# Instance norm in tiles: the last tile's statistics in one pass, and the end wait on another engine

## The chip, the cores and the metric

The kernel runs on one core of a Trainium2 chip. The metric is the device time of one execution in microseconds. A profile's "span" is some 1.7 us less than the time of the same execution. In profile lines PE is TensorE, DVE VectorE, ACT ScalarE, POOL GpSimd and SP SyncE; a q behind the name marks the engine's queue, where a transfer is issued. A transfer "lands" when the record of its end arrives. For the comparisons each kernel was run several times in turn with the kernel before, on the same chip.

Executions of the kernel before fall into two groups: of 59, 35 took 1246.70 to 1247.61 us (mean 1247.01) and 24 took 1249.23 to 1252.50, with nothing in between. I call them the **lower** and the **upper** group, and use the same split, at 1248, for the other kernels.

## The reference

```
mean = np.mean(x, axis=(2, 3, 4), keepdims=True)
var = np.var(x, axis=(2, 3, 4), keepdims=True)
return ((x - mean) / np.sqrt(var + eps)).astype(np.float32)
```

x has the shape (8, 64, 32, 64, 64) in fp32: 512 instances of 131072 elements, 268 MB, read once and written once.

## The kernel before

Two small parts come first, then 42 tiles of 128 partitions by 12288 columns, held in four slots of SBUF. A tile is three chunks of 4096 columns, and one instance is spread over 32 chunk rows; so each statistic is summed by partition, masked by chunk, summed over partitions by a matmul, and handed back to the chunks.

SyncE loads. VectorE and ScalarE each take part of the sums, then part of the squares about the mean, and scale. ScalarE issues the stores. Only the last tile's store goes in two pieces:

```python
    def tile_on_vector(eng, t, lane, c1, c3, c4, c16):
        ...
        for j, part in ((0, chunk[0]), (3, t[:, COLS - TURN :])):      # TURN = 1536
            eng.reduce_sum(out=column(a, SUMS, j), in_=part, axis=AXIS)...
        over_instance(eng, a, p[:, 0:12], SUMS, 4, MEANS, True, ...)   # mask, matmul, reduce, mask, reduce
        eng.tensor_scalar(out=chunk[0], in0=chunk[0], scalar1=column(a, MEANS, 0), ...)
        eng.tensor_tensor_reduce(out=unused[2][:], in0=chunk[0], in1=chunk[0], ..., accum_out=...)
        over_instance(eng, a, p[:, 12:21], SQUARES, 3, VARS, False, ...)
        eng.reciprocal(...)
        ... scale chunk[0], scale and shift chunk[1]

    def tile_on_scalar(eng, t, lane, c1, c3, c4, c16, dst, last=False):
        ... Identity with accum_out over chunk 1 and 2560 columns of chunk 2
        ... Square with bias = -mean and accum_out over chunks 1 and 2, then Sqrt
        if last:
            at = CHUNK
            eng.dma_start(out=dst[:, :at], in_=chunk[0])._wait_ge(done[lane], c3 - 2)...
        eng.activation(out=chunk[2], ..., scale=..., bias=...)
        eng.dma_start(out=dst[:, at:], in_=t[:, at:])._wait_ge(done[lane], c3)...

    def load_all(eng):                       # on SyncE
        ... all loads
        for k in range(n_tiles - SLOTS, n_tiles):
            uses = k // SLOTS + 1 + (k == n_tiles - 1)
            eng.wait_ge(stored[k % SLOTS], 16 * uses)
```

## Time and profile before

| | before |
|---|---|
| time | 1246.93 us, median of 3 (1246.81 to 1247.07) |
| span of the profile | 1245.6 us (its own execution took 1247.35) |
| moved | 536.9 MB, mean 431 GB/s |
| last load landed | 1206.11 us |
| first and second store of the last tile issued | 1225.70, 1229.92 us |
| last landing | 1244.34 us |

The last row is from the trace's records of DMA landings; the others are on the page and in the timeline. The prediction shows the lines and reads them.

### The profile page before, as it was taken

Reading aid. Unit: us, or ns where it says so; the run is one execution under the profiler, and the core shown is the slowest. Engines: PE = TensorE matmul, PEld = TensorE weight load, DVE = VectorE, ACT = ScalarE, POOL = GpSimd, SP = SyncE. Lnnn points to the kernel's source line nnn. Section 1 sums busy time; section 2 is a strip of 40 time slices with the busy share of each in tenths; the row PEclk is TensorE's granted clock in tenths of the full one; section 3 lists DMA queues with packets and bytes.
Section 4 is the critical chain, followed back from the end, with each engine's and each line's share of the span. In section 5 each row is a group of like instructions: output and inputs, shape, how many; then the busy total and the mean of one; then the engine's idle time right before and its main releaser. Section 6 shows DMA issues by size and latency. Waiting matters only on the chain.

```text
span 1245.6 us, 1951 instructions
## 1 busy us (share of the span) xinstructions
PE 52.6 (4%) x176; PEld 44.0 (4%) x176; DVE 811.4 (65%) x724; ACT 757.7 (61%) x433; POOL 2.7 (0%) x15
## 2 busy tenths in 40 slices
PE   0000000000000000000000000000000000000000
PEld 0000000000000000000000000000000000000000
DVE  2887666666666666666666666666666666666663
ACT  5776555666566666655556665666566555566653
POOL 0000000000000000000000000000000000000000
DMA  9999999999999999999999999999999999999998
GB/s 394 429 431 433 445 432 429 431 431 437 439 434 429 429 436 440 432 432 431 431 439 437 432 431 429 434 444 432 432 428 432 437 440 432 429 429 436 442 432 363
DMA packets 12818, 536.89 MB, mean 431 GB/s; under 512 B 1424, under 2 KB 1424, under 8 KB 1424
## 3 DMA queue, kind: packets, MB, share of 16 engines
q1 hardware_dynamic: 6336, 268.44, 49.9%
q10 hardware_dynamic: 6480, 268.44, 49.8%
q14 instruction: 2, 0.02, 0.0%
HBM read 268.44 MB, written 268.44 MB: 431 GB/s over the span
## 4 chain that ended last, share of the span: by engine, by line
another core or an unknown queue 82%; DMA 9%; ACT 3%; DVE 2%; SPq 1%; issue 1%; PE 0%; ACTq 0%
DMA slot<-in_x_dram 6%; DMA out_dram<-slot 4%; ACT unused L221 2%; SPq L364 1%; DVE small L157 1%; DVE slot L193 1%; ACT unused L214 0%; DVE slot L200 0%; ACT slot L240 0%; PE psum L257 0%; DVE small L137 0%; DVE small L125 0%; DVE small L131 0%; DVE small L143 0%
## 5 line engine op out<-in xcount | busy, mean ns | idle before, releaser
L214 ACT ACTIVATE unused<-slot 128x4096 uint8<-128x4096 f32 x84 | 249.3, 2968 | 310.8 <-DMA slot<-in_x_dram 308.4
L157 DVE TENSOR_REDUCE small<-slot 128x1 f32<-128x4096 f32 x84 | 255.3, 3081 | 280.0 <-DMA slot<-in_x_dram 280.0
L221 ACT ACTIVATE unused<-slot,small 128x4096 uint8<-128x4096 f32 x84 | 310.8, 3701 | 65.2 <-DVE small L143 65.2
L171 DVE CUSTOM_DVE_ANT_0 unused<-slot 128x4096 uint8<-128x4096 f32 x42 | 185.9, 4425 | 1.4
L240 ACT ACTIVATE slot<-slot,small 128x4096 f32<-128x4096 f32 x42 | 159.7, 3801 | 21.1 <-DVE small L188 18.0
L200 DVE TENSOR_SCALAR slot<-slot,small 128x4096 f32<-128x4096 f32 x42 | 101.1, 2407 | 0.0
L164 DVE TENSOR_SCALAR slot<-slot,small 128x4096 f32<-128x4096 f32 x42 | 98.8, 2353 | 1.5
L257 PE MATMUL psum<-small,avg 128*128 128x12 f32 (+1 forms) x168 | 50.3, 375 | 1144.6 <-DVE small L125 1144.6
L193 DVE TENSOR_SCALAR slot<-slot,small 128x4096 f32<-128x4096 f32 x42 | 98.6, 2347 | 0.0
L257 PEld LDWEIGHTS psum<-small,avg 128*128 128x128 f32 x168 | 42.0, 310 | 1152.8 <-DVE small L125 1152.8
L131 DVE TENSOR_REDUCE small<-psum 128x3 f32<-128x12 f32 x84 | 14.2, 169 | 58.0 <-PE psum L257 58.0
L228 ACT ACTIVATE small<-small,eps_t 128x3 f32<-128x3 f32 x42 | 12.5, 299 | 62.6 <-DVE small L143 62.6
L125 DVE TENSOR_TENSOR small<-small,belongs 128x12 f32<-128x12 f32 x84 | 14.2, 170 | 31.9 <-ACT unused L221 29.6
L185 DVE RECIPROCAL small<-small 128x3 f32<-128x3 f32 x42 | 7.4, 176 | 15.4 <-ACT small L228 15.4
L137 DVE TENSOR_TENSOR small<-small,belongs 128x9 f32<-128x9 f32 x84 | 14.3, 170 | 2.9
L221 ACT ACTIVATION_READ_ACCUMULATOR unused<-slot,small 128x1 f32 x84 | 15.7, 186 | 0.0
L214 ACT ACTIVATION_READ_ACCUMULATOR unused<-slot 128x1 f32 x84 | 15.6, 186 | 0.0
L143 DVE TENSOR_REDUCE small<-small 128x3 f32<-128x9 f32 x84 | 13.6, 162 | 2.9
L270 DVE TENSOR_REDUCE small<-slot 128x1 f32<-128x2048 f32 x2 | 4.6, 2284 | 9.0 <-DMA slot<-in_x_dram 9.0
L296 ACT ACTIVATE unused<-slot,small 128x4096 uint8<-128x4096 f32 x2 | 7.4, 3707 | 2.0 <-DVE small L273 2.0
L293 ACT ACTIVATE unused<-slot 128x2048 uint8<-128x2048 f32 x2 | 3.8, 1910 | 7.2 <-DMA slot<-in_x_dram 6.7
L188 DVE TENSOR_TENSOR small<-small 128x3 f32<-128x3 f32 x42 | 6.8, 162 | 1.4
(26 smaller groups left out, 21.1 us busy)
## 6 DMA issues: line engine op xcount, KB each, us to landing
slot<-in_x_dram SPq DMA_DIRECT2D x42, 6144.0 KB, 39.9
out_dram<-slot ACTq DMA_DIRECT2D x41, 6144.0 KB, 54.2
out_dram<-slot ACTq DMA_DIRECT2D x3, 2048.0 KB, 23.9
slot<-in_x_dram SPq DMA_DIRECT2D x2, 2048.0 KB, 10.2
out_dram<-slot ACTq DMA_DIRECT2D x1, 4096.0 KB, 14.4
```

What stands on the lines that cost most here:

```text
L125: eng.tensor_tensor(out=block(a, by_both, n, m), in0=spread(a, at, m), in1=belongs[:, :, :m], op=Alu.mult,)._wait_ge(*wait).then_inc(steps ...
L131: eng.tensor_reduce(out=a[:, by_instance : by_instance + n], in_=p.rearrange("p (n m) -> p n m", m=m), axis=AXIS, op=Alu.add,)._wait_ge(st ...
L137: eng.tensor_tensor(out=block(a, by_chunk, n, n), in0=spread(a, by_instance, n), in1=belongs[:, :, :n].rearrange("p i c -> p c i"), op=Alu ...
L157: eng.reduce_sum(out=column(a, SUMS, j), in_=part, axis=AXIS)._wait_ge(landed[lane], c16).then_inc(summed[lane], 1)
L164: eng.tensor_scalar(out=chunk[0], in0=chunk[0], scalar1=column(a, MEANS, 0), scalar2=None, op0=Alu.add,)._wait_ge(centred[lane], c1).then_ ...
L171: eng.tensor_tensor_reduce(out=unused[2][:], in0=chunk[0], in1=chunk[0], scale=1.0, scalar=0.0, op0=Alu.mult, op1=Alu.add, accum_out=colum ...
L193: eng.tensor_scalar(out=chunk[0], in0=chunk[0], scalar1=column(a, SCALES, 0), scalar2=None, op0=Alu.mult,)._wait_ge(scaled[lane], c1).then ...
L200: eng.tensor_scalar(out=chunk[1], in0=chunk[1], scalar1=column(a, SCALES, 1), scalar2=column(a, SHIFTS, 1), op0=Alu.mult, op1=Alu.add,)._w ...
L214: eng.activation(out=unused[j - 1][:, : part.shape[1]], in_=part, func=Act.Identity, accum_out=column(a, SUMS, j),)._wait_ge(landed[lane], ...
L221: eng.activation(out=unused[j - 1][:], in_=chunk[j], func=Act.Square, bias=column(a, MEANS, j), accum_out=column(a, SQUARES, j),)._wait_ge ...
L240: eng.activation(out=chunk[2], in_=chunk[2], func=Act.Identity, scale=column(a, SCALES, 2), bias=column(a, SHIFTS, 2),)._wait_ge(shifted[l ...
L257: eng.matmul(out=p[:, col : col + THIRDS * m], lhsT=avg[PART][:], rhs=a[:, at + m : at + m + THIRDS * m], start=True, stop=True,)._wait_ge ...
```

## The change

Its intent: in the last tile no later load hides the compute, so shorten it. VectorE takes means and variances of chunk 0 and 3360 columns of chunk 1 in one pass with bn_stats. ScalarE makes mean and spread of its own columns about its own mean, without waiting for the instance's. Both are combined from four pieces with weights by size. The wait for the last stores moves from SyncE to ScalarE. Cut to its core:

```diff
+    GROUP = 480
+    SHARE = 7 * GROUP
+    sizes = (CHUNK, SHARE, CHUNK, CHUNK - SHARE)
+    def last_on_vector(eng, t, lane, c1, c3, c4, c16):
+        for g, (at, size) in enumerate(groups):          # 8 of 512 columns, 7 of 480
+            i = eng.bn_stats(out=stats[:, g, :], in_=t[:, at : at + size])
+        step(eng.bn_aggr(out=a[:, 0:2], in_=stats[:, :split, :]))
+        step(eng.bn_aggr(out=a[:, 2:4], in_=stats[:, split:, :]))
+        weigh(means, BOTH); hand_out(0, ...)             # weights, matmul, reduce, mask, reduce
+        ... variances + (own mean - instance mean)^2, weigh, hand_out, reciprocal
+        ... scale and shift chunk 0, then chunk 1
+    def last_on_scalar(eng, t, lane, c1, c3, c4, c16, dst):
+        ... Identity with accum_out over 4096 and 736 columns: own means
+        ... Square about the own mean over the same columns, with accum_out
+        ... Sqrt, first store, scale and shift chunk 2, second store
@@ load_all
+    def wait_for_stores(eng):
         for k in range(n_tiles - SLOTS, n_tiles):
@@ set_up
+        ... 6 more small steps on GpSimd: belongs4 and weighs
@@ end
-    over_tiles(nc.vector, part_on_vector, tile_on_vector)
+    over_tiles(nc.vector, part_on_vector, tile_on_vector, last_on_vector)
+    wait_for_stores(nc.scalar)
```

More of the change, by code (lines that the diff above doesn't have):

```diff
@@ L72 @@
     belongs = sbuf("belongs", [P, THIRDS, THIRDS + 1])
+    GROUP = 480
+    SHARE = 7 * GROUP
+    first_of = (0, CHUNK, 2 * CHUNK, CHUNK + SHARE)
+    sizes = (CHUNK, SHARE, CHUNK, CHUNK - SHARE)
+    PIECES = len(sizes)
+    belongs4 = sbuf("belongs4", [P, THIRDS, PIECES])
+    weighs = sbuf("weighs", [P, THIRDS, PIECES])
+    groups = [(i * 512, 512) for i in range(CHUNK // 512)]
+    groups += [(CHUNK + i * GROUP, GROUP) for i in range(SHARE // GROUP)]
+    stats = sbuf("stats", [P, len(groups), 6])
+    late = sbuf("late", [P, 96])
     small = [sbuf(f"small{i}", [P, 72]) for i in range(LANES)]
@@ L97 @@
     moved = semaphores("moved", SLOTS)
+    went, meant, leaned, spread_, multiplied, took_root = semaphores("late", 6)
     sorted2 = semaphores("sorted2", SLOTS)
@@ L207, in tile_on_vector, with tile_on_scalar @@
         )._wait_ge(shifted[lane], c1).then_inc(done[lane], 1)
-    def tile_on_scalar(eng, t, lane, c1, c3, c4, c16, dst, last=False):
+    def tile_on_scalar(eng, t, lane, c1, c3, c4, c16, dst):
         a = small[lane]
@@ L233, in tile_on_scalar @@
         )._wait_ge(gathered[lane], c1).then_inc(rooted[lane], 1)
-        at = 0
-        if last:
-            at = CHUNK
-            eng.dma_start(out=dst[:, :at], in_=chunk[0])._wait_ge(
-                done[lane], c3 - 2
-            ).then_inc(stored[lane], 16)
         eng.activation(
@@ L246, in tile_on_scalar @@
         )._wait_ge(shifted[lane], c1).then_inc(done[lane], 1)
-        eng.dma_start(out=dst[:, at:], in_=t[:, at:])._wait_ge(done[lane], c3).then_inc(
+        eng.dma_start(out=dst, in_=t)._wait_ge(done[lane], c3).then_inc(
             stored[lane], 16
@@ L263, in tile_on_tensor, with step, weigh, hand_out @@
             )._wait_ge(before[lane], c1).then_inc(after[lane], 1)
+    BIAS, BOTH, INST, CHUNKED, NEGATIVE, FAR, FAR2, TOTAL = 8, 10, 22, 25, 37, 41, 45, 49
+    BOTH2, INST2, CHUNKED2, FOUND, ROOTED, SCALED, SHIFTED = 53, 65, 68, 77, 80, 83, 86
+    def last_on_vector(eng, t, lane, c1, c3, c4, c16):
+        a, p = late, psum[lane]
+        n, m = THIRDS, PIECES
+        means, variances = a[:, 0 : 2 * m : 2], a[:, 1 : 2 * m : 2]
+        count = 0
+        def step(i):
+            nonlocal count
+            if count:
+                i._wait_ge(went, count)
+            i.then_inc(went, 1)
+            count += 1
+        def weigh(what, to):
+            step(
+                eng.tensor_tensor(
+                    out=block(a, to, n, m),
+                    in0=what.unsqueeze(1).to_broadcast([P, n, m]),
+                    in1=weighs[:],
+                    op=Alu.mult,
+                )
+            )
+        def hand_out(col, inst, at, to, k, negate):
+            eng.tensor_reduce(
+                out=a[:, inst : inst + n],
+                in_=p[:, col : col + n * m].rearrange("p (n m) -> p n m", m=m),
+                axis=AXIS,
+                op=Alu.add,
+            )._wait_ge(multiplied, 1 if col == 0 else 2).then_inc(went, 1)
+            nonlocal count
+            count += 1
+            step(
+                eng.tensor_tensor(
+                    out=block(a, at, k, n),
+                    in0=a[:, inst : inst + n].unsqueeze(1).to_broadcast([P, k, n]),
+                    in1=belongs4[:, :, :k].rearrange("p i c -> p c i"),
+                    op=Alu.mult,
+                )
+            )
+            step(
+                eng.tensor_reduce(
+                    out=a[:, to : to + k],
+                    in_=block(a, at, k, n),
+                    axis=AXIS,
+                    op=Alu.add,
+                    negate=negate,
+                )
+            )
+        for g, (at, size) in enumerate(groups):
+            i = eng.bn_stats(out=stats[:, g, :], in_=t[:, at : at + size])
+            if g == 0:
+                i._wait_ge(landed[lane], c16)
+        i.then_inc(went, 1)
+        count += 1
+        split = CHUNK // 512
+        step(eng.bn_aggr(out=a[:, 0:2], in_=stats[:, :split, :]))
+        step(eng.bn_aggr(out=a[:, 2:4], in_=stats[:, split:, :]))
+        eng.wait_ge(meant, 2)
+        weigh(means, BOTH)
+        hand_out(0, INST, CHUNKED, NEGATIVE, m, True)
+        step(
+            eng.tensor_add(
+                out=a[:, FAR : FAR + m], in0=means, in1=a[:, NEGATIVE : NEGATIVE + m]
+            )
+        )
+        far = a[:, FAR : FAR + m]
+        step(eng.tensor_mul(out=a[:, FAR2 : FAR2 + m], in0=far, in1=far))
+        eng.wait_ge(spread_, 2)
+        step(
+            eng.tensor_add(
+                out=a[:, TOTAL : TOTAL + m], in0=variances, in1=a[:, FAR2 : FAR2 + m]
+            )
+        )
+        weigh(a[:, TOTAL : TOTAL + m], BOTH2)
+        hand_out(n * m, INST2, CHUNKED2, FOUND, n, False)
+        eng.wait_ge(took_root, 1)
+        step(
+            eng.reciprocal(out=a[:, SCALED : SCALED + n], in_=a[:, ROOTED : ROOTED + n])
+        )
+        step(
+            eng.tensor_mul(
+                out=a[:, SHIFTED : SHIFTED + n],
+                in0=a[:, NEGATIVE : NEGATIVE + n],
+                in1=a[:, SCALED : SCALED + n],
+            )
+        )
+        assert count == STEPS
+        for j in (0, 1):
+            part = t[:, j * CHUNK : (j + 1) * CHUNK]
+            eng.tensor_scalar(
+                out=part,
+                in0=part,
+                scalar1=column(a, SCALED, j),
+                scalar2=column(a, SHIFTED, j),
+                op0=Alu.mult,
+                op1=Alu.add,
+            )._wait_ge(went, STEPS).then_inc(done[lane], 1)
@@ new lines @@
+    WEIGHED, WEIGHED2, VARIED, STEPS = 4, 11, 14, 16
+    def last_on_scalar(eng, t, lane, c1, c3, c4, c16, dst):
+        a = late
+        mine = [(j, t[:, first_of[j] : first_of[j] + sizes[j]]) for j in (2, 3)]
+        for j, part in mine:
+            eng.activation(
+                out=unused[j - 2][:, : sizes[j]],
+                in_=part,
+                func=Act.Identity,
+                scale=1.0 / sizes[j],
+                accum_out=column(a, 0, 2 * j),
+            )._wait_ge(landed[lane], c16).then_inc(meant, 1)
+        for j, _ in mine:
+            eng.activation(
+                out=column(a, BIAS, j - 2),
+                in_=column(a, 0, 2 * j),
+                func=Act.Identity,
+                scale=-(sizes[j] ** -0.5),
+            )._wait_ge(meant, 2).then_inc(leaned, 1)
+        for j, part in mine:
+            eng.activation(
+                out=unused[j - 2][:, : sizes[j]],
+                in_=part,
+                func=Act.Square,
+                scale=sizes[j] ** -0.5,
+                bias=column(a, BIAS, j - 2),
+                accum_out=column(a, 0, 2 * j + 1),
+            )._wait_ge(leaned, 2).then_inc(spread_, 1)
+        eng.activation(
+            out=a[:, ROOTED : ROOTED + THIRDS],
+            in_=a[:, FOUND : FOUND + THIRDS],
+            func=Act.Sqrt,
+            bias=eps_t[:, 0:1],
+        )._wait_ge(went, VARIED).then_inc(took_root, 1)
+        eng.dma_start(out=dst[:, :CHUNK], in_=t[:, :CHUNK])._wait_ge(
+            done[lane], c3 - 2
+        ).then_inc(stored[lane], 16)
+        eng.activation(
+            out=t[:, 2 * CHUNK :],
+            in_=t[:, 2 * CHUNK :],
+            func=Act.Identity,
+            scale=column(a, SCALED, 2),
+            bias=column(a, SHIFTED, 2),
+        )._wait_ge(went, STEPS).then_inc(done[lane], 1)
+        eng.dma_start(out=dst[:, CHUNK:], in_=t[:, CHUNK:])._wait_ge(
+            done[lane], c3
+        ).then_inc(stored[lane], 16)
@@ L268, in part_on_vector, with last_on_tensor @@
+    def last_on_tensor(eng, t, lane, c1, c3, c4, c16):
+        for col, at, ready_at in ((0, BOTH, WEIGHED), (12, BOTH2, WEIGHED2)):
+            eng.matmul(
+                out=psum[lane][:, col : col + THIRDS * PIECES],
+                lhsT=avg[PART][:],
+                rhs=late[:, at : at + THIRDS * PIECES],
+                start=True,
+                stop=True,
+            )._wait_ge(went, ready_at).then_inc(multiplied, 1)
     def part_on_vector(eng, t, lane):
@@ L329, with over_tiles @@
     ]
-    def over_tiles(eng, on_part, on_tile, with_target=False):
+    def over_tiles(eng, on_part, on_tile, on_last, with_target=False):
         for m, (lane, t) in enumerate(parts):
@@ L348, in over_tiles @@
             c = k // SLOTS + 1
-            more = (out_t[k], k == n_tiles - 1) if with_target else ()
-            on_tile(eng, slots[k % SLOTS][:], k % SLOTS, c, 3 * c, 4 * c, 16 * c, *more)
+            more = (out_t[k],) if with_target else ()
+            step = on_last if k == n_tiles - 1 else on_tile
+            step(eng, slots[k % SLOTS][:], k % SLOTS, c, 3 * c, 4 * c, 16 * c, *more)
     def load_all(eng):
@@ L433, in set_up @@
         )
+        for to, c in ((slice(0, THIRDS), slice(0, THIRDS)), (slice(3, 4), slice(1, 2))):
+            step(eng.tensor_copy(out=belongs4[:, :, to], in_=belongs[:, :, c]))
+        for j, size in enumerate(sizes):
+            step(
+                eng.tensor_scalar(
+                    out=weighs[:, :, j : j + 1],
+                    in0=belongs4[:, :, j : j + 1],
+                    scalar1=float(size),
+                    scalar2=None,
+                    op0=Alu.mult,
+                )
+            )
         return count
@@ L438 @@
     nc.vector.wait_ge(ready, set_by)
-    over_tiles(nc.vector, part_on_vector, tile_on_vector)
+    over_tiles(nc.vector, part_on_vector, tile_on_vector, last_on_vector)
     nc.tensor.wait_ge(ready, set_by)
-    over_tiles(nc.tensor, part_on_tensor, tile_on_tensor)
+    over_tiles(nc.tensor, part_on_tensor, tile_on_tensor, last_on_tensor)
     nc.scalar.preload_act_table(Act.Sqrt)
     nc.scalar.wait_ge(ready, set_by)
-    over_tiles(nc.scalar, part_on_scalar, tile_on_scalar, with_target=True)
+    over_tiles(nc.scalar, part_on_scalar, tile_on_scalar, last_on_scalar, with_target=True)
+    wait_for_stores(nc.scalar)
 _INS = ['x', 'eps']
```

## The prediction

> **What bounds the kernel now.** I read first the page's rows of busy tenths, because the change touches one tile of 42 and so only the end of the span.
>
> ```profile
> DVE  2887666666666666666666666666666666666663
> ACT  5776555666566666655556665666566555566653
> DMA  9999999999999999999999999999999999999998
> DMA packets 12818, 536.89 MB, mean 431 GB/s; under 512 B 1424, under 2 KB 1424, under 8 KB 1424
> ```
>
> VectorE and ScalarE are busy six tenths, the DMA engines nine or more in every slice but the last. The kernel moves 536.9 MB and is bound by transfers. So the question is whether the end, where no more loads come, has another limit. The chain that ended last seems to say so: after the last load (landed at 1206.11) it runs through compute only.
>
> ```profile
> 1206.13 6.09 DVE small L157 x2
> ...
> 1213.71 7.50 ACT unused L221 x4
> ...
> 1223.40 2.28 DVE slot L193
> 1225.68 0.02 issue
> 1225.70 0.35 ACTq L237
> 1226.05 0.05 issue
> 1226.09 3.80 ACT slot L240
> ```
>
> The reader sees 19.57 us (1206.13 to 1225.70) from the landing to the first store of the last tile: two passes of sums and squares, 6.09 + 7.50 us, the small steps around them, and the scaling. The change shortens this. But that chain is of instructions, and stops at ScalarE's last one; it doesn't say whether the store, once issued, waits behind older stores. The busy table of the end does:
>
> ```profile
> core 0: us, PE busy (x) PEld busy (x) DVE busy (x) ACT busy (x) POOL busy (x), PEclk, DMA share, GB/s
> 1140.00:1198.96 58.96, 2.40 (x8) 2.00 (x8) 39.07 (x35) 35.31 (x21) 0.00 (x0) 1.00 0.99 430
> 1206.11:1241.20 35.09, 1.20 (x4) 1.00 (x4) 19.13 (x17) 17.62 (x10) 0.00 (x0) 1.00 0.99 427
> 1241.20:1245.60 4.40, 0.00 (x0) 0.00 (x0) 0.00 (x0) 0.00 (x0) 0.00 (x0) 1.00 0.09 37
> ```
>
> From the last landing to 1241.20 the DMA engines are as full (0.99, 427 GB/s) as in the steady part (0.99, 430), though nothing but stores is left. The reason is in the DMA issues:
>
> ```profile
> out_dram<-slot ACTq DMA_DIRECT2D x41, 6144.0 KB, 54.2
> out_dram<-slot ACTq DMA_DIRECT2D x1, 4096.0 KB, 14.4
> ```
>
> A store lands 54.2 us after its issue, while a tile of 6.29 MB needs 14.5 us at 433 GB/s: about two older stores are always queued. Counting the trace's packets from 1206.11 on, 15.14 MB are still to write: 6.29 are the last tile, 8.85 are the backlog of tiles 40 and 41. The backlog takes 8.85 / 0.433 = 20.4 us, to 1226.5. The last tile's first store is issued at 1225.70. Packet by packet, the first DMA engine ends its backlog at 1226.56 and goes on with the new store at once; sorted into 16 chains, no engine has a gap above 0.08 us from 1206 to its end. The compute chain is only just hidden, but it is hidden. The engines end at 1241.2 to 1243.9; the last one, never idle, sets the landing at 1244.34.
>
> **What the Trainium skill says.** "Perfetto Trace Analysis", section "Identifying the Most-Contended Engine", says to find the engine of highest occupancy and optimize that first: here the DMA, 0.99 even in the tail, which the change leaves alone. "DMA: Bandwidth & Descriptors", section "Specifications", gives 435 GB/s as the fabric's ceiling and about 358 as the HBM limit of a core; the trace agrees with the first (430 and 427) and is above the second. Its section "Queues, rings and completion order" says that an engine consumes descriptors in ring order; the trace agrees: packets of the new store start only after an engine's backlog ends. "VectorE: DVE Perf Modes", section "The perf-mode tier table", has tensor_reduce at one element per cycle and fp32 tensor_scalar at two; the trace agrees (4.42 us and 2.35 us for 4096 columns). I found no page with a cost for bn_stats, so I take the rate of tensor_reduce.
>
> **The change part by part** (times of the last tile, from its rows).
>
> VectorE's statistics. Removed: sums of 4096 and 1536 columns (6.09), the centring of chunk 0 (2.35), its squares (4.43) and one scaling of 2.35 that becomes a scale-and-shift (2.41). Added: bn_stats over 4096 + 3360 = 7456 columns in 15 instructions. Reductions of 4096 and 1536 columns take 4.419 and 1.743 us, so 1.045 ns per column and 0.14 us fixed, of which neighbours overlap about 0.08. Estimate: 7456 x 1.045 ns + 15 x 0.06 us = 8.7 us, to 1214.8. Two bn_aggr on small inputs, 0.24 each: 1215.3.
>
> ScalarE's statistics. Identity over 4096 takes 3.62 us and over 2560 takes 2.32, so 736 columns take 0.78; two tiny bias instructions of 0.3; Square over 4096 (3.71) and 736 (about 0.9) with accumulator reads. Sum about 9.8 us: done at 1215.9.
>
> Combining. Mask, matmul, reduce, mask, reduce took 1212.24 to 1213.71, 1.47 us; it is needed twice as before, now with no pass of data between. 1215.3 + 1.47 + two small steps 0.4 = 1217.2; ScalarE is done by then, so no wait. Add 0.2, combine 1.47, square root 0.33, reciprocal and product 0.4: 1219.6. Scaling chunk 0, 2.41: the first store is issued at about 1222.0 in place of 1225.70. ScalarE then scales chunk 2 (0.35 + 3.8), and the second store goes at about 1226.2 in place of 1229.92. So 3.7 us of the compute chain go. **Worth in time: none.** Both stores queue behind a backlog that is untouched, and at 1226.5 the engines go on with the same bytes at the same rate.
>
> Setup. Six GpSimd instructions more. The present ones end at 4.2 us, and take about 0.27 each including the handover; 4.2 + 6 x 0.27 = 5.8, before the first data at 9.02. Hidden.
>
> End wait. SyncE sees the last landing at 1244.36 and leaves 1.3 us of closing work to 1245.65. In the trace the other engines are released by SyncE's signal at 1244.59, and SyncE collects their answers from 1244.755 to 1244.82. With the wait on ScalarE, SyncE should already be in that collection, and only ScalarE's answer is missing. From 1244.39, the answer plus its handover should need about 0.1 where now 0.4 pass. Estimate: 0.3 us less. This is the only part on the path that sets the end.
>
> Sum: 1246.93 - 0 - 0 - 0.3 = **1246.6 us**.
>
> **Rivals.**
> 1. The compute chain sets the end after all; all 3.7 us arrive: 1246.93 - 3.7 - 0.3 = 1242.9. For it speaks the chain of instructions, and that the new store came only just in time. Against it: the share of 0.99 and the chains of packets without gaps. Even with all gaps closed the slowest engine had 37 us of its own packets to move after 1206.9. I give it 3 in 100.
> 2. bn_stats is slower than one column per cycle. At half the rate it takes 16.5 us, the first store goes 7.8 us later than I say, at 1229.8, and the engines stand idle some 4 us: about 1250.5. Nothing in this profile has measured bn_stats; 4 in 100.
> 3. Last DMA engine: one engine ends 1.2 us after the next (landings at 1244.34 and 1243.17). If queueing earlier changes which engine is behind, the end moves by some tenths either way. The same step (1.2 us) is seen at the landing of the store before, so I expect it to stay.
> 4. The end wait saves nothing, as both engines must meet in the closing barrier: 1246.9. Possible, 1 in 4; it lies in the range.
>
> **Range and chances.** The three runs before differ by 0.26 us. With the end wait's 0 to 0.4 and some tenths for rival 3, the range of 8 in 10 is 1245.9 to 1247.2. 2% is 25 us; no rival comes near: within 2% 0.98, the rest split.
>
> **What would show it.** In the changed kernel's timeline the first and second stores of the last tile are issued near 1222.0 and 1226.2, but land where they did, so their times to landing grow from 9.0 and 14.4 us to some 12.7 and 18. The DMA share stays about 0.99 from the last landing to 1241. bn_stats over 512 columns shows about 0.6 us each. The first data are still used at about 9.0 us. The closing work after the last landing shrinks from 1.3 to about 1.0 us. Wrong would make it: a landing of the first store well before 1234, or a gap of the DMA before it.

## The result, and the profile after

In the six first executions each, the changed kernel took 1247.00 us (median; 1246.76 to 1249.58), the kernel before 1246.91 (1246.78 to 1247.13). The ratio is 1.0004, 95% interval 0.9991 to 1.0017: the same. Ratios here are the mean time of one kernel's fast runs over that of the other's of the same rounds, so not quite the ratio of the medians.

The timeline of the changed kernel's last tile (start, duration, engine, line, operation, tiles) shows that the compute did get faster:

```profile
1205.96 8.76 DVE L332 BATCH_NORM_STATS2 stats<-slot 128x6 f32<-128x512 f32 x15 [7.21 <-DMA slot<-in_x_dram]
...
1214.53 0.89 ACT L405 ACTIVATE unused<-slot,late 128x736 uint8<-128x736 f32 x1
1214.75 0.37 DVE L338 BATCH_NORM_AGGREGATE late<-stats 128x2 f32<-128x48 f32 x1
...
1219.90 4.73 DVE L372 TENSOR_SCALAR slot<-slot,late 128x4096 f32<-128x4096 f32 x2
1222.35 0.35 ACTq L419 DMA_DIRECT2D out_dram<-slot  x1
1222.74 3.80 ACT L422 ACTIVATE slot<-slot,late 128x4096 f32<-128x4096 f32 x1 [3.35 <-DVE slot L372]
1226.57 0.34 ACTq L429 DMA_DIRECT2D out_dram<-slot  x1
```

Two passes have become one of 8.76 us on VectorE; ScalarE is through at 1215.5, in time. The stores are issued 3.35 us earlier by the clock of the span. What became of that stands in the landing times. First the changed kernel's issue of the 4 MB store (name, queue, count, size, us to landing), then the first store's line from its source view:

```profile
out_dram<-slot ACTq DMA_DIRECT2D x1, 4096.0 KB, 17.6
```

```profile
DMA to landing us min/median/max: 12.2/12.2/12.2
```

Before, these were 14.4 and 9.0 us. Each store now waits 3.2 us longer for its landing: all that it gained, as the chain from the last load's landing to the first issue is 3.18 us shorter. The busy table of the changed kernel's end, with the last two columns DMA share and GB/s, is the twin of the one before:

```profile
1140.00:1198.78 58.78, 2.40 (x8) 2.00 (x8) 38.89 (x35) 35.24 (x20) 0.00 (x0) 1.00 0.99 430
1205.96:1241.00 35.04, 1.21 (x4) 1.00 (x4) 16.41 (x32) 13.59 (x12) 0.00 (x0) 1.00 0.99 427
1241.00:1245.30 4.30, 0.00 (x0) 0.00 (x0) 0.00 (x0) 0.00 (x0) 0.00 (x0) 1.00 0.07 30
```

VectorE's busy time after the last load fell from 19.13 to 16.41 us and ScalarE's from 17.62 to 13.59, and the DMA share stayed 0.99. The saving was of time that lay beside the transfers.

### The profile page after: what moved, and what is told of

The parts are those of the page before. It is cut to its first block, busy times and chain, and to the rows that moved or that the text cites. A ratio compares the mean times of both kernels' runs of the same rounds, so it can differ in the third digit from the quotient of the medians.

```text
span 1245.3 us, 1977 instructions
## 1 busy us (share of the span) xinstructions
PE 52.7 (4%) x176; PEld 44.1 (4%) x176; DVE 808.7 (65%) x739; ACT 753.7 (61%) x435; POOL 4.0 (0%) x21
## 4 chain that ended last, share of the span: by engine, by line
another core or an unknown queue 82%; DMA 9%; DVE 3%; ACT 2%; SPq 1%; issue 1%; PE 0%; ACTq 0%; DVEq 0%
DMA slot<-in_x_dram 6%; DMA out_dram<-slot 4%; ACT unused L236 1%; SPq L543 1%; DVE stats L332 1%; DVE small L173 0%; ACT unused L229 0%; DVE slot L216 0%; DVE slot L209 0%; ACT slot L422 0%; PE psum L266 0%; DVE slot L372 0%; PE psum L435 0%; SPq L541 0%
## 5 line engine op out<-in xcount | busy, mean ns | idle before, releaser
L229 ACT ACTIVATE unused<-slot 128x4096 uint8<-128x4096 f32 x82 | 243.4, 2968 | 302.9 <-DMA slot<-in_x_dram 300.5
L173 DVE TENSOR_REDUCE small<-slot 128x1 f32<-128x4096 f32 x82 | 249.2, 3081 | 272.8 <-DMA slot<-in_x_dram 272.8
L236 ACT ACTIVATE unused<-slot,small 128x4096 uint8<-128x4096 f32 x82 | 303.4, 3701 | 63.7 <-DVE small L159 63.7
L187 DVE CUSTOM_DVE_ANT_0 unused<-slot 128x4096 uint8<-128x4096 f32 x41 | 181.4, 4426 | 1.4
L249 ACT ACTIVATE slot<-slot,small 128x4096 f32<-128x4096 f32 x41 | 155.9, 3801 | 18.0 <-DVE small L204 18.0
L216 DVE TENSOR_SCALAR slot<-slot,small 128x4096 f32<-128x4096 f32 x41 | 98.7, 2406 | 0.0
L180 DVE TENSOR_SCALAR slot<-slot,small 128x4096 f32<-128x4096 f32 x41 | 96.5, 2353 | 1.5
L266 PE MATMUL psum<-small,avg 128*128 128x9 f32 (+1 forms) x164 | 49.1, 375 | 1116.7 <-DVE small L141 1116.7
L209 DVE TENSOR_SCALAR slot<-slot,small 128x4096 f32<-128x4096 f32 x41 | 96.2, 2346 | 0.0
L332 DVE BATCH_NORM_STATS2 stats<-slot 128x6 f32<-128x512 f32 (+1 forms) x15 | 8.8, 662 | 7.2 <-DMA slot<-in_x_dram 7.2
L390 ACT ACTIVATE unused<-slot 128x4096 uint8<-128x4096 f32 (+1 forms) x2 | 4.4, 2208 | 8.0 <-DMA slot<-in_x_dram 8.0
L474 ACT ACTIVATE unused<-slot,small 128x4096 uint8<-128x4096 f32 x2 | 7.4, 3707 | 2.0 <-DVE small L451 2.0
## 6 DMA issues: line engine op xcount, KB each, us to landing
out_dram<-slot ACTq DMA_DIRECT2D x41, 6144.0 KB, 54.2
```

The source lines that it names most:

```text
L216: eng.tensor_scalar(out=chunk[1], in0=chunk[1], scalar1=column(a, SCALES, 1), scalar2=column(a, SHIFTS, 1), op0=Alu.mult, op1=Alu.add,)._w ...
L229: eng.activation(out=unused[j - 1][:, : part.shape[1]], in_=part, func=Act.Identity, accum_out=column(a, SUMS, j),)._wait_ge(landed[lane], ...
L236: eng.activation(out=unused[j - 1][:], in_=chunk[j], func=Act.Square, bias=column(a, MEANS, j), accum_out=column(a, SQUARES, j),)._wait_ge ...
L249: eng.activation(out=chunk[2], in_=chunk[2], func=Act.Identity, scale=column(a, SCALES, 2), bias=column(a, SHIFTS, 2),)._wait_ge(shifted[l ...
L266: eng.matmul(out=p[:, col : col + THIRDS * m], lhsT=avg[PART][:], rhs=a[:, at + m : at + m + THIRDS * m], start=True, stop=True,)._wait_ge ...
L332: i = eng.bn_stats(out=stats[:, g, :], in_=t[:, at : at + size])
```

## The experiments

My theory: the stores of earlier tiles keep the DMA engines busy until after the last tile's stores are issued, so the last tile's chain has slack, and its length matters only beyond that. Rival A: the chain sets the end. Rival B: the slack is unlimited, as only bytes count. A second question is what the end wait is worth.

The load of the last tile lands at other times in each execution (1205.6 to 1209.1 in the profiles), mostly 2 to 3 us later in the upper group. So profiles of different groups are compared from that landing on. This table gathers them; its columns are worked out from the traces' landing records, the timeline and the span:

| kernel | last load's landing | to the first store's issue | to the end of the span | closing work |
|---|---|---|---|---|
| before | 1206.11 | 19.59 | 39.54 | 1.306 |
| changed | 1205.93 | 16.41 | 39.36 | 1.103 |
| end wait alone | 1208.76 | 19.59 | 39.20 | 1.102 |
| new statistics alone | 1207.85 | 16.41 | 39.56 | 1.306 |
| changed, one extra sum | 1206.81 | 20.22 | 39.40 | 1.103 |
| before, one extra sum | 1209.05 | 23.46 | 40.78 | 1.306 |
| changed, two extra sums | 1205.95 | 24.54 | 41.67 | 1.103 |
| before, store cut | 1205.61 | 19.59 | 36.92 | 1.306 |
| changed, store cut | 1208.24 | 16.41 | 33.54 | 1.102 |

"Closing work" is from the last landing to the end of the span.

The landing records also show what the upper group is. The last load has one landing for each of the 16 DMA engines. In two profiles of the changed kernel, at 1247.00 and 1249.59 us, the mean of these landings is nearly the same, 1203.88 and 1204.09, but the last of them comes at 1205.93 and 1208.65. At the end of the last store it is the same again: means 1241.99 and 1242.20, last 1244.19 and 1246.75. So in the slower execution one engine is further behind, and the others are not. Why it falls behind isn't shown.

### The two halves of the change alone

```diff
# end wait alone: the kernel before, and
+    def wait_for_stores(eng): ...
+    wait_for_stores(nc.scalar)
# new statistics alone: the changed kernel, and
-    wait_for_stores(nc.scalar)
+    wait_for_stores(nc.sync)
```

> The kernel before with the end wait moved from SyncE to ScalarE and nothing else. If the end wait is the only part on the path that sets the end (my theory, as predicted): the closing work after the last landing shrinks from 1.3 us to about 1.1 (1.10 in the profile of the changed kernel), time 0.2 us under the kernel before, 1246.7. Rival: what the closing work gains is inside the noise or is given back outside of the span, time as before within 0.1 us.

> The change with the end wait put back on SyncE: the new statistics alone. Theory (the stores queue behind the backlog): first and second store issued near 1222.3 and 1226.6 as in the changed kernel, landings at about 1234.6 and 1244.3 as before, closing work 1.3 us, time as before within 0.2 us, 1246.9. Rival (the compute chain sets the end): 3.4 us less, 1243.5.

The end wait alone took 1247.29 us (median of 5, 1246.80 to 1249.65), ratio 0.9993 (0.9979 to 1.0007). The new statistics alone took 1248.63 (median of 6, 1247.38 to 1250.01), ratio 1.0004 (0.9991 to 1.0018). Many of these executions were of the upper group, so 0.2 us can't be read from them; but Rival A's 3.4 us can: it is not there. From the landing of the last load to the end the new statistics alone need 39.56 us, the kernel before 39.54, with the first store 3.18 us earlier. The closing work is 1.306 us with the wait on SyncE and 1.102 or 1.103 with it on ScalarE, in all 18 profiles.

The profiles of the upper group sharpen the theory. In the one of the end wait alone, with its old statistics, the last load lands late and so does the first store's issue, at 1228.35 us; most engines have ended their backlog by then and stand idle. In one of the changed kernel (the run at 1249.59 us, reported below) the store is issued at 1225.06, in time. First the end wait alone, then the changed kernel:

```profile
1226.80:1228.20 1.40, 0.00 (x0) 0.00 (x0) 1.40 (x1) 0.00 (x0) 0.00 (x0) 1.00 0.08 35
```

```profile
1226.80:1228.20 1.40, 0.00 (x0) 0.00 (x0) 0.55 (x1) 1.40 (x1) 0.00 (x0) 1.00 0.79 339
```

Both need 39.2 us from the last load's landing to the end, although the share is 0.08 in one and 0.79 in the other. In both the engine that ends last never ran out of packets. So it is this engine that hides the chain, and not that all of them are full.

### Using up the slack

A sum over 4096 columns that nobody reads is put on VectorE ahead of the last tile's scaling:

```diff
# before, one extra sum (last tile only)
+        eng.reduce_sum(out=a[:, 70:71], in_=chunk[0], axis=AXIS)
         eng.reciprocal(out=a[:, SCALES : SCALES + 3], ...)
# changed, one (two) extra sums
+        eng.reduce_sum(out=a[:, 95:96], in_=t[:, :CHUNK], axis=AXIS)
         eng.wait_ge(took_root, 1)
```

> The kernel before with one extra sum over 4096 columns on VectorE ahead of the last tile's scaling, 4.42 us of which some 0.4 hide behind the square root: the first store is issued at about 1229.8 in place of 1225.7. Theory: the engines that end their backlog at 1226.6 stand idle 4 us, but the one that ends last (landing at 1229.8, so its data at 1229.4) idles only from 1229.4 to about 1230.8; the end moves by 1.4 to 2 us, not by 4: about 1248.6. Rival (the compute chain sets the end): plus 4.0 us, 1250.9. A rival of pure backlog, with a lot of slack: no change.

> The changed kernel with the same extra sum of 4.42 us (some 4.0 of it not hidden): first store issued at about 1226.4, so 0.7 us later than in the kernel before. Theory: the 3.4 us that the change saved are slack and are what is used up here; the slowest DMA engine is not reached and the time stays as that of the changed kernel within 0.2 us, 1247.0. Rival (the compute chain sets the end): plus 4.0, 1251.0.

> The changed kernel with two extra sums, 8.84 us of which 8.4 are not hidden: first store at about 1230.8, 5.1 us later than in the kernel before. Theory: the slowest DMA engine, free at about 1229.4, waits until about 1231.8: plus 2.4 us, and the other engines then end at 1246.4 too: 1249.5 to 1250. Rival (the chain sets the end): plus 8.4, 1255.4.

Changed with one extra sum: 1248.16 us (median of 6, 1247.10 to 1249.92), ratio 1.0002 (0.9988 to 1.0016); its two quickest executions, 1247.10 and 1247.18, lie among those of the changed kernel. A chain 3.81 us longer (20.22 against 16.41) moved the end by 0.04 us. Before with one extra sum: 1249.04 (1248.08 to 1251.57), ratio 1.0008 (0.9994 to 1.0022), three of six at 1248.08 to 1248.65. There a chain 3.87 us longer moved the end by 1.24. Changed with two: 1249.32 (1249.27 to 1249.36, all four), ratio 1.0014 (0.9998 to 1.0029): 8.13 us longer, 2.30 us later. So neither rival holds. Not all of the length arrives, against A; and some of it does once the slack is used up, against B.

The busy table of the kernel before with one extra sum shows the slack's end (the last two columns are the DMA share and GB/s):

```profile
1209.00:1226.00 17.00, 1.20 (x4) 1.00 (x4) 14.60 (x14) 13.82 (x9) 0.00 (x0) 1.00 0.98 422
1229.00:1232.00 3.00, 0.00 (x0) 0.00 (x0) 2.97 (x4) 0.00 (x0) 0.00 (x0) 1.00 0.04 16
1233.50:1248.00 14.50, 0.00 (x0) 0.00 (x0) 1.30 (x1) 3.21 (x1) 0.00 (x0) 1.00 0.97 417
```

Now all 16 engines are idle before the first store, which is issued at 1232.51. Sorting the packets into 16 chains, the engines idle between 1.1 and 7.1 us there: most end their backlog at 1226.4 to 1227.3, one only at 1232.28. The 1.1 us of this last one are close to the 1.24 that the end moved, where the others' 4 to 7 us cost nothing more: they would have waited at the end for the last one.

### Taking the backlog away

The store of the last tile but one is cut to 128 of its 12288 columns, in both kernels. Their outputs are wrong, which doesn't matter for the times.

```diff
-        eng.dma_start(out=dst, in_=t)...
+        to = COLS if keep is None else keep          # keep = 128 for tile n_tiles - 2
+        eng.dma_start(out=dst[:, :to], in_=t[:, :to])...
```

> The kernel before, but the store of the last tile but one is cut from 12288 columns to 128 (its output is wrong on purpose), which takes 6.2 MB or 14.4 us of the backlog away. Theory: the queue then runs empty at about 1212 to 1215, long ahead of the first store at 1225.7, so that compute chain sets the end: 6.29 MB from about 1226.7 take 14.5 us to 1241.2, landing near 1241.7, and 1.3 us of closing work: span about 1243.0, time 1244.2 to 1245. It gains only 2 to 3 of the 14.4 us, since the chain was hidden only just. Rival (transfers alone count): 14 us less, 1232.5.

> The changed kernel with the same store cut (output wrong on purpose). Theory: now nothing hides the last tile's chain, so the change is worth what it saves of it: first store at 1222.4 in place of 1225.7, and the time is 3.2 to 3.6 us under that of the kernel before with the same cut: about 1241. Rival (the change is worth nothing even then, for example because the stores themselves are slower): the same time as the kernel before with the cut.

The kernel before with the cut took 1244.24 us (median of 5, 1244.14 to 1244.67), ratio 0.9974 (0.9960 to 0.9988): it lost 14.4 us of transfers and gained under 3. The changed kernel with the cut took 1241.73 in its one execution of the lower kind and 1243.48 to 1244.26 in the other four, median 1243.59, ratio 0.9966 (0.9952 to 0.9979). By the medians the expected 3.2 to 3.6 us are missed: the gain is 0.65. The profile says where the rest is: in it the last load landed at 1208.24, and at 1205.61 in the other kernel's (why, isn't shown). From that landing on, 36.92 us became 33.54: 3.38 less, which are the chain's 3.18 and the closing work's 0.20. First the busy table of the kernel before with the cut, then that of the changed kernel with it:

```profile
1205.60:1212.00 6.40, 0.03 (x1) 0.03 (x1) 6.25 (x3) 6.03 (x4) 0.00 (x0) 1.00 0.91 392
1214.50:1226.00 11.50, 0.60 (x2) 0.50 (x2) 9.61 (x11) 6.91 (x6) 0.00 (x0) 1.00 0.00 0
1226.20:1240.70 14.50, 0.00 (x0) 0.00 (x0) 1.29 (x1) 3.19 (x1) 0.00 (x0) 1.00 0.97 416
```

```profile
1208.20:1212.00 3.80, 0.00 (x0) 0.00 (x0) 3.73 (x7) 3.73 (x3) 0.00 (x0) 1.00 0.99 427
1217.20:1225.00 7.80, 1.21 (x4) 1.00 (x4) 5.57 (x17) 0.93 (x3) 0.00 (x0) 1.00 0.00 0
1225.60:1240.20 14.60, 0.00 (x0) 0.00 (x0) 1.35 (x1) 3.25 (x1) 0.00 (x0) 1.00 0.98 417
```

In both, the engines move nothing for several microseconds (share 0.00) while VectorE and ScalarE work, and then need 14.5 us for the last tile. Here the chain sets the end, and from the last load's landing on the change is worth all that it saves. In the real kernel the same chain lies beside 14.4 us more of stores.

### What became of the end wait's 0.2 us

The closing work is 0.20 us shorter in every profile, yet the changed kernel is not quicker. I ran it and its halves again:

> The changed kernel again, to settle whether the 0.20 us that its closing work is shorter (1.103 us against 1.306 in every profile so far, by where the end wait stands) reach the time. In the undisturbed executions (before: 1246.77 to 1247.14) theory: 0.2 us under before. Rival: no difference, because the time in which the last DMA engine lands scatters by as much.

> The end wait alone, again, for more undisturbed executions. Theory: as the changed kernel, 0.2 us under before. Rival: as before.

> The new statistics alone, again; so far it has one undisturbed execution (1247.38) against eight each of the changed kernel (mean 1247.0) and of the end wait alone (mean 1246.86). Theory (only the end wait counts, 0.2 us): as before, 1247.0. Rival (the new statistics cost what the end wait saves): 1247.2, 0.2 us over before.

> The end wait alone, for more undisturbed executions on the same chip as the run before this. Theory and rival both: 0.2 us under before, 1246.8.

> The changed kernel on the same chip. Theory: 0.2 us under before, 1246.8. Rival: as before, 1247.0.

The changed kernel: 1247.05 (median of 5) and 1247.02 (of 5), ratios 0.9997 and 0.9994. The end wait alone: 1246.83 (of 6) twice, ratios 0.9996 and 1.0001. The new statistics alone: 1247.35 (of 5), ratio 0.9996. These intervals span about 0.0027, some 3 us, as the upper group falls unevenly, so no ratio decides. The means of the lower group alone, over all comparisons, with the standard error:

| kernel | executions below 1248 us | mean |
|---|---|---|
| before | 35 of 59 | 1247.01 ± 0.04 |
| end wait alone | 13 of 23 | 1246.88 ± 0.08 |
| changed | 13 of 16 | 1247.01 ± 0.03 |
| new statistics alone | 6 of 11 | 1247.41 ± 0.10 |

The new statistics, with the wait left alone, are 0.4 us over before. That seems to speak for the rival, that they cost what the wait saves. But the means don't add up: 0.4 less 0.2 would leave the changed kernel 0.2 us over before, and it is level. The end wait alone gains 0.13 ± 0.09, so its 0.20 is not shown in the time either. These means also hang on the split at 1248: with the executions up to 1248.59 counted in, the end wait alone has 1247.08 and the new statistics alone 1247.59.

The profiles show where the 0.2 us are and where they are not. From the last load's landing to the end, the eight profiles with the wait on ScalarE, whole output and no extra work at the end take 39.20 to 39.39 us, and the three with it on SyncE 39.54 to 39.56. So the gain is there. More scatter lies ahead of it, in when the last load lands: 1205.71 to 1206.63 in the profiles of the lower group. The one profile of the new statistics alone in that group has the latest, 1206.63. No new statistics have run by then, and the mean over its 16 engines, 1203.82, is no later than before (1204.01): again it is one engine that is behind. So a cost of the new statistics is not shown. Ahead of that landing the change adds only six set-up steps on GpSimd, and tables in SBUF. A last pair tried the set-up alone on top of the end wait:

```diff
# the end wait alone, and
+        ... step(eng.tensor_copy(out=belongs4...)) twice, step(eng.tensor_scalar(out=weighs...)) four times
```

> The end wait moved, and the change's six extra set-up instructions on GpSimd (their tables are made and not used); the last tile as before. So far, undisturbed executions: before 1247.0, end wait alone 1246.82, the whole change 1247.01, new statistics alone 1247.35. If the set-up is what costs the 0.2 to 0.3 us: 1247.0. If it lies in the last tile's code: 1246.8.

> The end wait alone, on the chip of the run before this, as its yardstick: 1246.8.

This pair decided nothing: 1249.92 us (median of 6, 1246.99 to 1250.32), ratio 0.9998 (0.9982 to 1.0014), and 1250.31 (1247.64 to 1252.37), ratio 1.0005 (0.9987 to 1.0022), one execution of each in the lower group. It stays open whether the new statistics' 0.4 us are more than the last engine's lag; they are 0.03% of the time, and rest on 6 executions.

### Which DMA engine ends last

If one and the same DMA engine were always last, the last store could give it less to do. Behind the last store 16 tiny loads of 1 to 16 rows were issued:

```diff
+    for n in range(1, 17):
+        nc.scalar.dma_start(out=probe[:n, ...], in_=x_t[0][:n, :4]).then_inc(probed[n - 1], 16)
     wait_for_stores(nc.scalar)
```

> The changed kernel with 16 tiny loads of 1 to 16 rows issued behind the last store on the same queue, each with a semaphore of its own: a load of n rows should run on n DMA engines, and its landings tell when each of these engines is through with its stores. Theory: one engine lands 1 to 2.5 us behind the next, and the load whose landings first show it names the engine. Rival: the lag is spread evenly. Time within 0.3 us of the changed kernel.

> The same tiny loads behind the kernel with only the end wait moved. Theory: the same engine is last as in the run before this. Rival: another one is, so that no fixed split of the last store could level the ends.

One execution each: 1249.61 and 1252.53 us. The tiny loads end 2.3 and 2.6 us after the last store and made these two slower, so neither counts as a time. The load of n rows had n landings (besides a record at its issue); each load repeats the landings of the one before, 0.2 us later, with one new engine. So the order tells the engine. Landings of the first loads, in us:

```
changed:  1 row 1241.56 | 2 rows 1241.75, 1242.81 | 4 rows ..., 1243.43 | 5 rows ..., 1244.75
before:   1 row 1244.70 | 2 rows 1244.88, 1247.30 | 3 rows ..., 1247.47
```

In the first run the fifth engine is last; in the second the second engine is, 2.4 us behind the first. The rival holds as far as two executions go, one of each kernel: another engine was last, and a fixed split made for one would not have levelled the other. No version that beats both kernels by more than the scatter came out of this.

## Why the prediction was right or wrong

**What bounds the kernel: right.** The new chain passed its saving to the queue; landings came nearly where they did before (1234.52 and 1244.19 against 1234.67 and 1244.34; the last load had landed 0.17 us earlier), and cutting the backlog brought the saving out. One reading on the way was off: "about two older stores are always queued". A store is issued every 29 us and lands after 54.2, so one older store is ahead of it. The sum isn't touched, as it counts the bytes from the packets.

**Times of the parts: close.** bn_stats took 8.76 us against 8.7, bn_aggr 0.37 and 0.34 against 0.24, the first store 1222.35 against 1222.0, the second 1226.57 against 1226.2. So the chain lost 3.18 us from the last load's landing, not 3.7.

**Slack: understated.** I wrote that the chain was "only just hidden". That holds for the first DMA engine to run dry, at 1226.56. For the last one there was more: the changed kernel with an extra sum issued its first store 0.63 us later after the landing than the kernel before, and its last landing was later by 0.06 us only. So Rival 2 was too dear as well: it put a first store at 1229.8 at "about 1250.5", and with two extra sums it went at 1230.49 and the kernel took 1249.32. And in the upper group most engines did run dry (share 0.08 above), at no cost from the last load's landing on.

**The end wait: the term that was mis-sized.** The step "Estimate: 0.3 us less" measured 0.20 (1.306 to 1.103). I had set "the answer plus its handover" at 0.1 us, where 0.4 passed. In the trace it takes 0.28 us, from the end of ScalarE's wait (1244.255) to SyncE's going on (1244.536); before, SyncE needed 0.50 (1244.386 to 1244.886).

**The sum: the step that failed.** "1246.93 - 0 - 0 - 0.3" takes the end wait for "the only part on the path that sets the end", and so carries it whole into the time. Of the 0.3 us, 0.20 exist, from the last load's landing on; in the time nothing shows: both kernels have the mean 1247.01 in the lower group. When the last load lands is on that path too, and it varied by 0.9 us between the profiles of the lower group. Whether this scatter alone hides the 0.20, or the new statistics ("Worth in time: none") cost some of it ahead of that landing, stays open. Rival 4, "The end wait saves nothing", described the outcome, but not for its reason: the closing work did shrink. That the measured time lies so near the forecast is no credit to the 0.3 us; a forecast of 1246.9, no change, would have been the honest reading of an effect no larger than the scatter of the runs.

**Rival 3: wrong.** It said of the last engine's lag of 1.2 us behind the next: "so I expect it to stay". In the eleven profiles with whole output and no extra work at the end it was 0.07 to 2.98 us. This lag makes the difference between the two executions of the changed kernel compared above, 2.6 us, far more than any term of the sum.

## What to carry to other kernels

The chain that ended last is a chain of instructions; before shortening it, ask at the end of the kernel how many bytes are still queued ahead of the store that it releases, and divide by the rate. Do so for each DMA engine where the trace allows it, as the one that ends last decides. Here the saving in front of the queue showed as a longer time from issue to landing and nowhere else. To see whether a saving is real but hidden, cut the backlog in both kernels: here it then came out whole, counted from the last load's landing.

## What the Trainium skill lacked or had wrong

- "VectorE: DVE Perf Modes" has no cost for bn_stats or bn_aggr. Fifteen BATCH_NORM_STATS2 over 7456 columns took 8.76 us, 1.17 ns per column with all overheads, near the rate of tensor_reduce; BATCH_NORM_AGGREGATE over 48 and 42 inputs took 0.37 and 0.34 us.
- "DMA: Bandwidth & Descriptors", section "Specifications", gives about 358 GB/s as the HBM limit of a core. Here 430 GB/s went in the steady part, and 427 with stores alone. This kernel runs on one core; the row does not say that the figure is for two cores that share a memory stack, as the page's section "Bandwidth" does.
- The same section gives about 0.6 us from issue to first byte for transfers issued by SyncE or ScalarE, and not from where it is counted. From the start of the first load's issue to its first packet the trace has 1.03 us (1.033 to 2.067). The issuing instruction itself takes 0.39 of them; from its end it is 0.65, which agrees.
- No page that I found has the scatter between DMA engines that sets the end here: in two executions of one kernel the mean of the 16 engines' last landings was 1241.99 and 1242.20 us, and the last one 1244.19 and 1246.75.
